# Turning retention's, attention's and the mixed result's blocks by transposing DMAs, with the mixing's first two column blocks summed pair by pair and fewer accumulating transfers

## The chip, the cores and the metric

One core of a Trainium2 chip runs the whole layer as one program. The metric is the device time of that program in microseconds (us). The profile comes from one execution of it.

## The reference, cut to what matters

The layer works on 256 tokens of 2048 features in float32: a half feed-forward (SwiGLU, 5632 wide), two token mixers side by side, a projection of their gated sum, a second half feed-forward, and a gated embedding. Only the parts that the change touches are quoted:

```python
def reference(...):
    h = layer_norm(alpha * h + 0.5 * swiglu(h, w_ffn1_gu, w_ffn1_down), ...)
    rq, rk, rv, rg, aq, ak, av, gate_r, gate_a = split(h @ w_in)
    ...
    ro = head_group_norm(retention_chunkwise(rq, rk, rv), ret_gn_g)        # 8 heads of 256
    ret_branch = (silu(rg) * ro) @ w_ret_out
    att_branch = sliding_window_attention_sinks(aq, ak, av, sinks) @ w_att_out   # 16 heads of 64
    mixed = (sigmoid(gate_r) * ret_branch + sigmoid(gate_a) * att_branch) @ w_mix_out
    h = layer_norm(alpha * h + mixed, ...)
    h = layer_norm(alpha * h + 0.5 * swiglu(h, w_ffn2_gu, w_ffn2_down), ...)
    ...
```

`swiglu(h)` is `(silu(g) * u) @ w_down`, where g and u are the two halves of `h @ w_gu`.

## The kernel before

**Products.** Every float32 operand of a large product is held as two float32r parts, a rounded one (hi) and the rest (lo). `Sum.add` (lines 387 to 396) issues three matmuls for one product of a 128x128 by a 128x512 block: lo by hi, hi by hi, hi by lo. A weight chunk is 128 x 1024 (512 KB). `Single` loads one through SyncE's queue (line 113) and makes hi by a copy on ScalarE (line 99) and lo by a subtraction on VectorE (line 100). `Folded` makes lo without VectorE: ScalarE writes hi and then minus hi (lines 163 and 164), and an accumulating DMA that GpSimd issues adds the raw weights to that (line 165). `Seven` forms a product of two chunks with seven block products in place of eight, for which VectorE forms sums of the weights; `Prepared` is the same with sums that were formed earlier and stored away. One chunk of a plain product occupies TensorE with 12 matmuls, a `Seven` with 21.

**The order of the weights.** `plan` lists the chunks in the order of use. `fill` (line 280) runs after each chunk is used up: it has chunks made while under 45 matmuls of work stand ready, and loaded while under 90 are under way, as far as the room in SBUF goes. A stage's order is a string of letters: P is a pair of `Single` chunks, F is a `Single` and a `Folded`, S is a `Seven`, D a `Prepared`. `gu_units` (line 874) gives the order of each of the eleven groups of a feed-forward's first product. In the first feed-forward groups 1 to 10 are `FFSSFSSF`. In the second, groups 6, 8, 9 and 10 are `FFSSFSSP`, groups 4, 5 and 7 begin with `FF` and hold D, groups 1 to 3 hold no F.

**Side work.** Small jobs stand in a list, `side`. After each chunk `run_side` takes one job from it, so a job n places down the list is issued n chunks later. Engines take their own instructions in the order of issue, and SyncE's queue does the same with its loads.

**Turns.** A product needs its left operand with features on the partitions. Four stages turn a result from tokens on partitions to that form.
- A feed-forward's activations (`turned`, line 929) go by a DMA. ScalarE parts the float32 words into two planes of 16 bits (line 935), SyncE issues a transposing DMA of 16 blocks of 128x128 (line 939), and ScalarE joins the two planes to float32 again (line 948). The DMA is issued at the next chunk and the joining three chunks later.
- Retention turns each head by four TensorE transposes against an identity (line 1268, tile `rt`). ScalarE and VectorE read the result from PSUM (lines 1279 and 1280) and write the two parts `rett`. One list of side jobs for two heads has ten places.
- Attention turns the weights of two heads by six such transposes (line 1387, tile `at`) four chunks after the scores (tile `as`), and ScalarE copies them out (line 1390). `att3` multiplies them with the values (tile `ao`, lines 1403 and 1404). For the last pair of heads it comes seven chunks after the scores.
- The mixed result (`sig`) is turned by four times four transposes for each half (line 1470, tile `mxt`). Each is split into `mixt`, the left operand of the mixing's product `mo`. The first half is turned beside the second half's retention product (`mr1`). The second half is turned beside the beginning of `mo`.

**Mixing.** The product `mo` has four column blocks of 512. Each runs through all 16 blocks of features before the next begins, 8 chunks for each column block. The two accumulators of a block are read once it is done (line 1509).

Of the kernel before, what the change touches and what calls it, by code (L numbers as in the profile page):

```python
# [8 lines left out]
F32 = mybir.dt.float32  # L9
# [35 lines left out]
AHEAD_SLOTS = 32  # L45

# [10 lines left out]
def layer(ctx: ExitStack, tc: tile.TileContext, io):  # L57
# [90 lines left out]
    class Folded:  # L148
# [11 lines left out]
        def make(self):  # L160
            c = self.chunk
            c.make_hi()
            act.copy(c.hi, c.raw)
            act.mul(c.lo, c.hi.bitcast(F32), -1.0)
            pool.dma_start(c.lo, c.raw, accum_op=ALU.add)  # L165

# [752 lines left out]
    def ffn(name, i, ht, norm, keep, residual, keepers, away):  # L919
# [9 lines left out]
        def turned(j, v):  # L929


            words = slot([P, 2, 2, 512], U16, f"{name}w{j}")
            of_v = v.bitcast(U16).rearrange("p t (n h) -> p h t n", h=2)
            for h in range(2):
                act.copy(words[:, h], of_v[:, h])
            moved = slot([P, 2, 2, 4, P], U16, f"{name}m{j}")

            def turn():
                sync.dma_start_transpose(
                    moved.rearrange("p h t k n -> p (h t k) n"), words.rearrange("p h t n -> p (h t n)")  # L940
                )

            def joined():
                raw = slot([P, 4, S], F32, f"{name}a{j}")
                raws.append(raw)
                of_raw = raw.bitcast(U16).rearrange("p k (t n h) -> p h t k n", t=2, h=2)
                for h in range(2):
                    act.copy(of_raw[:, h], moved[:, h])

            later(0, turn)  # L950
            later(3, joined)
# [165 lines left out]
    gate_keys = lambda b: lambda n, p: ("w_in_f2", 29 + 4 * b + 2 * n, p)  # L1117
    ret_keys = lambda b: lambda n, p: ("w_ret2", 4 * b + 2 * n, p)

    def plan_mixers():  # L1120
        plan_tokens(("w_rv", 0), KD)
        for grp in range(8):
            plan_features([("w_in_f", grp)], KD)
        for blk in range(1, 4):
            plan_tokens(("w_rv", blk), KD)
        for grp in range(8, 16, 2):
            plan_tokens(("w_in_f2", grp), KD)
        plan_tokens(("w_av",), KD, nk=4)
# [10 lines left out]
        for blk in range(4):  # L1139
            plan_tokens(("w_mix", blk), KD)  # L1140
# [7 lines left out]
    def mixers(ht, norm, residual, keepers, away):  # L1148
# [48 lines left out]
        ret_t = [None] * HR  # L1197
        gate_v = [None] * HR
# [43 lines left out]
        def ret2b(h):  # L1242
            def f():
# [3 lines left out]
                o = half(f"ron{h}")  # L1247
# [4 lines left out]
                keep["o", h] = o  # L1252

            return f

        def ret2c(h):
            def f():
                o = keep["o", h]
                dve.tensor_tensor(o, o, gate_v[h], ALU.mult)
            return f  # L1260

        def ret3(h):
            def f():
                o = keep.pop(("o", h))
                ps = bank(f"rt{h}").rearrange("p (a b) -> p a b", a=2)
                for e in range(2):
                    for t in range(2):
                        pe.transpose(ps[:, e, t * P : (t + 1) * P], o[:, t, e * P : (e + 1) * P], ident)
                keep["r", h] = ps
            return f  # L1270

        def ret3b(h):
            def f():
                ps = keep.pop(("r", h))
                ret_t[h] = slot([P, 2, 512], F32R, f"rett{h}")
                for e in range(2):
                    gk = gn[:, 2 * h + e : 2 * h + e + 1]
                    hi, lo = ret_t[h][:, e, :S], ret_t[h][:, e, S:]
                    act.mul(hi, ps[:, e, :S], gk)
                    dve.scalar_tensor_tensor(lo, ps[:, e, :S], gk, hi, ALU.mult, ALU.subtract)  # L1280
            return f
# [11 lines left out]
        for h in range(0, HR, 2):  # L1293
# [6 lines left out]
            for e in range(2):  # L1300
                gate_v[h + e] = g[:, :, e * DV : (e + 1) * DV]
# [79 lines left out]
        def att2(m):  # L1381
            def f():
                s = keep.pop(("p", m))
                ps = banks(f"at{m}")
                for e in range(2):
                    for j in range(3):
                        pe.transpose(ps[e][:, j * P : (j + 1) * P], s[:, e, j * P : (j + 1) * P], ident)
                pt = slot([P, 2, 384], F32, f"apt{m}")
                for e in range(2):
                    act.copy(pt[:, e], ps[e][:, :384])  # L1390
                keep["pt", m] = pt
            return f
# [71 lines left out]
        def turned(v, kk):  # L1464
            mt = slot([P, 2, 512], F32R, f"mixt{len(mix_t)}")
            mix_t.append(mt)
            ps = bank(f"mxt{len(mix_t)}").rearrange("p (a b) -> p a b", a=2)
            for j in range(2):
                for t in range(2):
                    pe.transpose(ps[:, j, t * P : (t + 1) * P], v[:, t, (kk + j) * P : (kk + j + 1) * P], ident)  # L1470
            split(mt[:, :, :S], mt[:, :, S:], ps)
# [11 lines left out]
        for b in range(2):  # L1483
# [7 lines left out]
            side.append(idle)  # L1491
            side.extend(lambda v=v, kk=kk: turned(v, kk) for v in sig[2 * b : 2 * b + 2] for kk in (0, 2))
# [9 lines left out]
        for blk in range(3):  # L1502
            if blk == 2:
                load_for_norm(1)
            ps = banks(f"mo{blk}")
            y[blk] = load_columns(residual, blk, "mixy")
            tokens_out(("w_mix", blk), KD, lhs, ps)
            for t in range(2):
                dve.scalar_tensor_tensor(y[blk][:, t], y[blk][:, t], ALPHA, ps[t], ALU.mult, ALU.add)
            block_stats(stats, y, blk)  # L1510
        y[3] = load_columns(residual, 3, "mixy")
# [318 lines left out]
```

## Time and profile before

| | us |
|---|---|
| median of 3 runs | 2260.68 (2256.12 to 2261.04) |
| the profiled execution | 2257.79 |
| its span, first to last instruction | 2255.8 |
| ScalarE busy in the span | 1366.8 (61%) |
| VectorE busy in the span | 1960.8 (87%) |

A row of a group gives the line, the engine, the operation, the tile written and those read, shapes and count, then the busy time in us and the mean time of one in ns, then the idle time of the engine before these instructions and what ended it. A row of the timeline gives the start, the duration, and in brackets an idle time before it with what ended that. A row of a stretch gives for each engine the busy time and the number of instructions, then the granted TensorE clock, the share of the 16 DMA engines in use, and GB/s. TensorE's matmuls overlap, so the cost of one is read from the distance between starts and not from its duration.

### The profile page before, as it was taken

The page shows a single profiled execution, that of the slowest core. Times are in us where ns is not written, and L with a number is a line of the kernel's source. Part 1 is how long each engine was busy: PE and PEld are TensorE (multiplying, and loading weights), DVE is VectorE, ACT ScalarE, POOL GpSimd, SP SyncE. Part 2 cuts the span into 40 slices and gives each one's busy share as a digit, 9 for nine tenths or more (in the row PEclk, how much of TensorE's full clock was granted, in tenths as well). Part 3 has the DMA queues.
Part 4 walks back from the last instruction along what each step waited for, and adds up shares of the span by engine and source line. Part 5 has one row for each costly group of instructions (what it writes and reads, how often), then busy time and mean ns, then how long its engine had stood idle before and what let it go on. Part 6 is the DMA issues. An engine that isn't in the chain of part 4 may idle for free.

```text
span 2255.8 us, 29093 instructions
## 1 busy us (share of the span) xinstructions
PE 2241.5 (99%) x10303; PEld 1857.3 (82%) x10303; DVE 1960.8 (87%) x2564; ACT 1366.8 (61%) x1607; POOL 52.6 (2%) x67
## 2 busy tenths in 40 slices
PE   9999999999999999999999999999999999999998
PEld 8888888788888888888778888888887788888887
DVE  6999989999988887888789788689998899889887
ACT  6787877766554453535556454455777677655533
POOL 0010010000000000000000000000000000000000
PEclk9999999999999999999999999999999999999999
DMA  9999999965677878775456568787999998555772
GB/s 319 257 288 250 280 274 247 276 218 181 225 284 273 282 289 287 252 240 175 139 157 229 182 214 291 274 295 260 306 292 300 299 249 265 195 210 208 290 264 74
DMA packets 265241, 557.66 MB, mean 247 GB/s; under 512 B 63100, under 2 KB 67580, under 8 KB 265096
## 3 DMA queue, kind: packets, MB, share of 16 engines
q1 hardware_dynamic: 254760, 522.82, 68.7%
q0 software_dynamic: 8352, 30.41, 7.0%
q10 hardware_dynamic: 1984, 2.58, 0.4%
q8 instruction: 81, 1.33, 0.2%
q14 instruction: 64, 0.52, 0.1%
HBM read 484.43 MB, written 29.36 MB: 228 GB/s over the span
## 4 chain that ended last, share of the span: by engine, by line
PE 90%; DMA 5%; issue 2%; DVE 2%; ACT 1%; ACTq 0%; POOLq 0%; SPq 0%; DVEq 0%
DMA lf_gu<-rf_gu 3%; PE rqk L345 3%; PE f1g L394 2%; PE f1g L396 2%; PE f1g L395 2%; PE f1u L396 2%; PE f1u L395 2%; PE f1u L394 2%; PE f2g L396 2%; PE f2g L395 2%; PE f2g L394 2%; DMA rf_gu<-in_f_gu 2%; PE f2u L396 2%; PE f2u L395 2%; PE f2u L394 2%
## 5 line engine op out<-in xcount | busy, mean ns | idle before, releaser
L100 DVE TENSOR_TENSOR lf_gu<-rf_gu,hf_gu 128x1024 fp32r<-128x1024 f32 (+1 forms) x210 | 250.2, 1208 | 15.5 <-ACT hf_gu L99 14.7
L99 ACT CAST hf_gu<-rf_gu 128x1024 fp32r<-128x1024 f32 (+1 forms) x210 | 214.4, 1038 | 33.6 <-DMA rf_gu<-in_f_gu 32.2
L100 DVE TENSOR_TENSOR lf_down<-rf_down,hf_down 128x1024 fp32r<-128x1024 f32 x150 | 178.8, 1219 | 18.4 <-ACT hf_down L99 17.2
L100 DVE TENSOR_TENSOR lw_in_f<-rw_in_f,hw_in_f 128x1024 fp32r<-128x1024 f32 x140 | 167.4, 1218 | 25.0 <-ACT hw_in_f L99 24.7
L99 ACT CAST hf_down<-rf_down 128x1024 fp32r<-128x1024 f32 x150 | 151.9, 1050 | 51.9 <-DMA rf_down<-in_f_down 22.3
L99 ACT CAST hw_in_f<-rw_in_f 128x1024 fp32r<-128x1024 f32 x140 | 140.2, 1051 | 2.9 <-PE rv L395 1.4
L99 ACT CAST huf_gu<-uf_gu 128x1024 fp32r<-128x1024 f32 x76 | 80.1, 1054 | 95.8 <-DVE uf_gu L191 94.1
L99 ACT CAST hvf_gu<-vf_gu 128x1024 fp32r<-128x1024 f32 x76 | 80.1, 1054 | 32.5 <-DVE vf_gu L193 31.5
L165 POOL DMA_DIRECT2D lf_gu<-rf_gu x58 | 50.2, 866 | 1845.9 <-DMA rf_gu<-in_f_gu 1253.0
L100 DVE TENSOR_TENSOR luf_gu<-uf_gu,huf_gu 128x1024 fp32r<-128x1024 f32 x76 | 92.5, 1217 | 0.0
L100 DVE TENSOR_TENSOR lvf_gu<-vf_gu,hvf_gu 128x1024 fp32r<-128x1024 f32 x76 | 92.5, 1217 | 0.0
L394 PE MATMUL f1g<-hf_gu,xt 128*128 128x512 f32 x232 | 90.5, 390 | 0.2 <-ACT hf_gu L99 0.2
L396 PE MATMUL f1g<-lf_gu,xt 128*128 128x512 f32 x232 | 90.5, 390 | 0.0
L395 PE MATMUL f1g<-hf_gu,xt 128*128 128x512 f32 x232 | 90.3, 389 | 0.0
L394 PE MATMUL f2g<-hf_gu,ht 128*128 128x512 f32 x214 | 83.4, 390 | 0.0
L396 PE MATMUL f2g<-lf_gu,ht 128*128 128x512 f32 x214 | 83.3, 389 | 0.0
L395 PE MATMUL f2g<-hf_gu,ht 128*128 128x512 f32 x214 | 83.3, 389 | 0.0
L396 PE MATMUL f1u<-lf_gu,xt 128*128 128x512 f32 x192 | 75.3, 392 | 2.4 <-DMA lf_gu<-rf_gu 2.4
L394 PE MATMUL f1u<-hf_gu,xt 128*128 128x512 f32 x192 | 74.7, 389 | 0.0
L395 PE MATMUL f1u<-hf_gu,xt 128*128 128x512 f32 x192 | 74.7, 389 | 0.0
L396 PE MATMUL f2u<-lf_gu,ht 128*128 128x512 f32 x168 | 66.0, 393 | 4.5 <-DMA lf_gu<-rf_gu 4.5
L394 PE MATMUL f2u<-hf_gu,ht 128*128 128x512 f32 x168 | 65.8, 391 | 0.0
(1464 smaller groups left out, 6796.5 us busy)
## 6 DMA issues: line engine op xcount, KB each, us to landing
rf_gu<-in_f_gu SPq DMA_DIRECT2D x360, 512.0 KB
rf_down<-in_f_down SPq DMA_DIRECT2D x176, 512.0 KB
rw_in_f<-in_w_in_f SPq DMA_DIRECT2D x148, 512.0 KB
lf_gu<-rf_gu POOLq DMA_DIRECT2D x58, 512.0 KB, 7.8
rw_rv<-in_w_rv SPq DMA_DIRECT2D x32, 512.0 KB
rw_ret<-in_w_ret SPq DMA_DIRECT2D x32, 512.0 KB
rw_mix<-in_w_mix SPq DMA_DIRECT2D x32, 512.0 KB
rw_pg<-in_w_pg SPq DMA_DIRECT2D x32, 512.0 KB
```

The costliest lines, as they stand in the source:

```text
L99: act.copy(dst_hi, src)
L100: (lo_engine or dve).tensor_tensor(dst_lo, src, dst_hi, ALU.subtract)
L165: pool.dma_start(c.lo, c.raw, accum_op=ALU.add)
L345: pe.matmul(ps[f], hi[:, kk, f * P : (f + 1) * P], rhs(k), start=k == 0, stop=k == n_k - 1,)
L394: pe.matmul(o, al, bh, start=first, stop=False)
L395: pe.matmul(o, ah, bh, start=False, stop=False)
L396: pe.matmul(o, ah, bl, start=False, stop=self.left == 0)
```

## The change

The DMA turn becomes a class, `Turn`, with `part` (two ScalarE copies), `move` (the transposing DMA on SyncE's queue) and `join` or `join_rows` (two ScalarE copies). Retention, attention and the mixed result use it in place of TensorE's transposes: one turn for two heads of retention (4 in all, 16 blocks each), one for two heads of attention (8, 12 blocks each), one for 512 columns of the mixed result (4, 16 blocks each). The 112 TensorE transposes of these stages are gone. In retention and the mixed result ScalarE and VectorE then read the joined tile in SBUF where they read PSUM.

In retention, `move` is issued two chunks before `join`, in attention too, and in the mixed result as well. In the feed-forwards `move` is issued one chunk later than before (`DELAY`), and the joining one chunk later too.

The mixing's first two column blocks are summed together: each pair of features is multiplied with both blocks' chunks before the next pair, with four accumulators held. Their readings come after the sixteenth chunk.

Of the `Folded` chunks 15 of 58 become `Single`. These are the last F of each of groups 1 to 10 in the first feed-forward (now `FFSSFSSP`), and in the second the first F of groups 4, 5 and 7 and of groups 6 and 8 (now `PFSSFSSP`).

```diff
+DELAY = 1
+    class Turn:
+        def __init__(self, src, name):
+            self.a, self.b = src.shape[1], src.shape[2] // P
+            self.src, self.name = src, name
+        def part(self):
+            of_src = self.src.bitcast(U16).rearrange("p a (n h) -> p h a n", h=2)
+            self.words = slot([P, 2, self.a, self.b * P], U16, "w" + self.name)
+            for h in range(2):
+                act.copy(self.words[:, h], of_src[:, h])
+        def move(self):
+            self.moved = slot([P, 2, self.a, self.b, P], U16, "m" + self.name)
+            sync.dma_start_transpose(
+                self.moved.rearrange("p h a b n -> p (h a b) n"), self.words.rearrange("p h a n -> p (h a n)")
+            )
+        def join(self, dst):
+            of_dst = dst.bitcast(U16).rearrange("p b (a n h) -> p h a b n", a=self.a, h=2)
+            for h in range(2):
+                act.copy(of_dst[:, h], self.moved[:, h])
...
-            return units_of(*((f"{plain * 2}SDSDSP", SEVEN[:3]) if j % 2 else (f"{plain * 2}SSDSSP", SEVEN)), AHEAD[j])
-        order = "FFSSFSSP" if name == "f2" else "FFSSFSSF"
+            return units_of(*((f"P{plain}SDSDSP", SEVEN[:3]) if j % 2 else (f"P{plain}SSDSSP", SEVEN)), AHEAD[j])
+        order = "FFSSFSSP" if name == "f1" or j > 8 else "PFSSFSSP"
...
-            later(0, turn)
-            later(3, joined)
+            later(DELAY, turn.move)
+            later(DELAY + 3, joined)
...
+    MIX_UNITS = [("P", p) for p in range(KD // 2)]
+    mix_keys = lambda n, p: ("w_mix", n, p)
...
-            side.append(ret2c(h))
-            side.append(ret2c(h + 1))
-            side.append(ret3(h))
-            side.append(both(ret3b(h), ret3(h + 1)))
-            side.append(ret3b(h + 1))
+            c = h // 2
+            side.extend((ret2c(c), ret3(c), ret3a(c), idle, ret3b(c)))
...
-            for j, part in ((0, att1), (1, att1b), (2, att1c), (4, att2)):
+            for j, part in ((0, att1), (1, att1b), (2, att1c), (3, att2), (4, att2a), (6, att2b)):
...
-            side.append(idle)
-            side.extend(lambda v=v, kk=kk: turned(v, kk) for v in sig[2 * b : 2 * b + 2] for kk in (0, 2))
+            t0, t1 = (Turn(v, f"mx{2 * b + n}") for n, v in enumerate(sig[2 * b : 2 * b + 2]))
+            side.extend((
+                t0.part, lambda t0=t0, t1=t1: (t0.move(), t1.part()), t1.move,
+                lambda t0=t0: split_turned(t0), lambda t1=t1: split_turned(t1),
+            ))
...
+        pm = [banks(f"mo{blk}") for blk in range(2)]
+        block("mo0", MIX_UNITS, mix_keys, lhs, None, [[Sum(pm[n][t], KD) for n in range(2)] for t in range(2)], None, before_mix)
+        for blk in range(2):
+            residual_added(blk, pm[blk])
```

`ret3`, `ret3a` and `ret3b` call `part`, `move` and `join`, `att2`, `att2a` and `att2b` do the same with `join_rows`. `split_turned` joins and then splits into two tiles of `mixt`.

More of the change, by code (lines that the diff above doesn't have):

```diff
@@ L165, in make, with join_rows @@
             pool.dma_start(c.lo, c.raw, accum_op=ALU.add)
+    class Turn:
[16 more added lines that the diff above has]
+                act.copy(of_dst[:, h], self.moved[:, h])
+        def join_rows(self, dst):
+            of_dst = dst.bitcast(U16).rearrange("p a (n h) -> p h a n", h=2)
+            for h in range(2):
+                act.copy(of_dst[:, h], self.moved[:, h].rearrange("p a b n -> p a (b n)"))
     class Seven:
@@ L929, in turned @@
         def turned(j, v):
[L932 to L941, printed above, removed]
-            def joined():
[L944 to L948, printed above, removed]
-            later(0, turn)
-            later(3, joined)
+            turn = Turn(v, f"{name}{j}")
+            turn.part()
+            def joined():
+                raws.append(slot([P, 4, S], F32, f"{name}a{j}"))
+                turn.join(raws[-1])
+            later(DELAY, turn.move)
+            later(DELAY + 3, joined)
         acts = {}
@@ L1138, in plan_mixers @@
             block_units(RET_UNITS, ret_keys(b))
-        for blk in range(4):
+        block_units(MIX_UNITS, mix_keys)
+        for blk in range(2, 4):
             plan_tokens(("w_mix", blk), KD)
@@ L1195, in mixers @@
             values(blk, ps)
[L1197 to L1198 removed]
+        ret_t, gate_v = [], []
         keep = {}
@@ L1382, in f, with att2a, att2b @@
             def f():
[L1383 to L1391, printed above, removed]
+                keep["t", m] = Turn(keep.pop(("p", m)), f"at{m}")
+                keep["t", m].part()
+            return f
+        def att2a(m):
+            return lambda: keep["t", m].move()
+        def att2b(m):
+            def f():
+                keep["pt", m] = slot([P, 2, 384], F32, f"apt{m}")
+                keep.pop(("t", m)).join_rows(keep["pt", m])
             return f
@@ L1462, in of_pairs, with split_turned @@
             return a[:, :S], a[:, S:]
[L1464 to L1471, printed above, removed]
+        def split_turned(turn):
+            raw = slot([P, 4, S], F32, f"mixr{len(mix_t)}")
+            turn.join(raw)
+            for j in (0, 2):
+                mt = slot([P, 2, 512], F32R, f"mixt{len(mix_t)}")
+                mix_t.append(mt)
+                split(mt[:, :, :S], mt[:, :, S:], raw[:, j : j + 2])
         slots_for_weights(20)
@@ L1501, in mixers, with residual_added @@
         lazy.append(sums_ahead(ahead[8:], 3, 2))
[L1502 to L1507, printed above, removed]
+        def residual_added(blk, ps):
             for t in range(2):
```

54 lines of the change are left out of this document (30 added, 24 removed).

## The prediction

> **What bounds the kernel now.** I read the page's first part, then the slices, then who waited for whom on TensorE, then the groups of the transposes on TensorE.
>
> ```profile
> span 2255.8 us, 29093 instructions
> ## 1 busy us (share of the span) xinstructions
> PE 2241.5 (99%) x10303; PEld 1857.3 (82%) x10303; DVE 1960.8 (87%) x2564; ACT 1366.8 (61%) x1607; POOL 52.6 (2%) x67
> ## 2 busy tenths in 40 slices
> PE   9999999999999999999999999999999999999998
> ```
> ```profile
> PE f2u L396 <- DMA lf_gu<-rf_gu: 4.5, 5, 1.7
> PE f1u L396 <- DMA lf_gu<-rf_gu: 2.4, 4, 1.1
> ```
>
> TensorE (PE) is busy in 2241.5 of 2255.8 us and in every slice. So the time can only come from work taken off TensorE and from its few stops. Nearly all stops inside the span are of one kind: a matmul waits for the lo part of a `Folded` chunk, which an accumulating DMA writes, nine times for 6.9 us in all. VectorE is at 87% and must stay behind TensorE. ScalarE, at 61%, has room.
>
> **The transposes on TensorE.** These are the groups that go, and four rows of the timeline round one set of four:
>
> ```profile
> L1387 PE MATMUL at<-ident,asc 128*128 128x128 f32 x48 | 6.8, 277 | 0.0
> L1268 PE MATMUL rt<-ident,ron 128*128 128x128 f32 x32 | 4.8, 272 | 0.0
> L1470 PE MATMUL mxt<-ident,sig 128*128 128x128 f32 x32 | 4.8, 272 | 0.0
> ```
> ```profile
> 1375.48 0.39 PE L396 MATMUL mo<-lw_mix,mixt 128*128 128x512 f32 x1
> 1375.71 0.60 PE L1470 MATMUL mxt<-ident,sig 128*128 128x128 f32 x4
> 1376.06 0.47 PE L394 MATMUL mo<-hw_mix,mixt 128*128 128x512 f32 x1
> 1376.38 0.39 PE L395 MATMUL mo<-hw_mix,mixt 128*128 128x512 f32 x1
> ```
>
> A row's duration overlaps the next, so I count starts. From 1375.48 to 1376.38 lie 0.90 us, in which two matmuls also begin. A matmul takes 0.23 from start to start (1375.48 to 1375.71), so two take 0.46 and four transposes 0.44 us, 0.11 each. The bare distance, 0.35 for four, gives 0.09. At 0.11 the 32 + 32 of retention and the mixed result give 7.0 us, the 48 of attention 5.3, **12.3 us** together (10.1 at 0.09). The groups' own busy times, 6.8 + 4.8 + 4.8 = 16.4, overlap their neighbours and are the upper bound. TensorE has no gap in these stages (the stretches below), so what it no longer issues comes off the end, if nothing else becomes late.
>
> **What takes their place.** ScalarE, SyncE's queue and the DMAs. The feed-forwards' turns show the prices:
>
> ```profile
> L948 ACT COPY f1a<-f1m x22: 1347/1355/1366, 70.1 to 480.9; 128x1024 uint16<-128x1024 uint16 x22
> L939 SPq DMA_TRANSPOSE f1m<-f1w x11: 1322/1874/3547, 57.5 to 468.0; - x11
> ...
> L935 ACT COPY f1w<-evw x20: 1036/1041/1044, 96.7 to 467.0; 128x1024 uint16<-128x1024 uint16 x20
> ```
> ```profile
> 905.00:1018.00 113.00, 113.00 (x621) 98.12 (x621) 95.67 (x196) 51.20 (x70) 0.00 (x0) 1.00 0.75 251
> 1030.00:1160.00 130.00, 130.00 (x684) 103.59 (x683) 98.43 (x189) 73.30 (x157) 0.00 (x0) 1.00 0.48 150
> 1325.00:1400.00 75.00, 75.00 (x347) 62.05 (x347) 67.52 (x75) 37.00 (x43) 0.00 (x0) 1.00 0.71 240
> 86.00:127.00 41.00, 41.00 (x182) 33.83 (x181) 37.40 (x46) 31.84 (x35) 3.46 (x4) 1.00 0.92 262
> 1712.00:1753.00 41.00, 39.30 (x172) 31.92 (x171) 40.11 (x49) 31.85 (x34) 3.47 (x4) 1.00 0.94 269
> 1835.00:1876.00 41.00, 41.00 (x182) 33.97 (x181) 38.59 (x47) 30.89 (x33) 2.40 (x4) 1.00 0.90 255
> ```
>
> The columns are TensorE, weight loads, VectorE, ScalarE, GpSimd, clock, DMA share and GB/s; the first three rows are retention's, attention's and the mixed result's turns. A turn of 16 blocks costs ScalarE 2 x 1.04 to part and 2 x 1.355 to join, 4.8 us; one of attention's 12 blocks three quarters, 3.6. Retention's four add 19 us, attention's eight 29, the mixed result's four 19. ScalarE is idle for 62, 57 and 38 us of these stretches, and attention's old copies out of PSUM go as well. VectorE gets no new instruction here. SyncE's queue is held 1.3 to 3.5 us by each of 16 issues (30 us at the median of 1.87), and its loads are issued up to 90 matmuls, some 20 us, ahead. So none of it fills an engine; what counts is when a turn arrives.
>
> The trace shows no row for the landing of a transposing DMA. From below it is the issue, 1.9 us. From above, the first joining started at 70.1 after the issue at 57.5 and waited for nothing, so 12.6. Of the same 512 KB, SBUF to SBUF, is the accumulating transfer, and I take its landing:
>
> ```profile
> lf_gu<-rf_gu POOLq DMA_DIRECT2D x58, 512.0 KB, 7.8
> ```
>
> The joining is issued two chunks after the DMA, 2 x 12 x 0.227 = 5.4 us. At 7.8 ScalarE then waits some 2.4 us, with the next chunks' copies queued behind it, and VectorE's subtractions after those. Chunks are made up to 45 matmuls ahead, 10.2 us. 2.4 of waiting and 2.7 of joining stay below that, so I cost it at nothing, with this cover named.
>
> Two places have a deadline of their own.
>
> ```profile
> 1372.33 1.23 DVE L1490 TENSOR_TENSOR sig<-sig,eve 128x1024 f32<-128x1024 f32 x1
> ...
> L394 PE MATMUL mo<-hw_mix,mixt x128: 389/389/481, 1370.3 to 1458.5; 128*128 128x512 f32 x128
> ...
> L99 ACT CAST mixt<-mxt x8: 578/587/595, 1332.3 to 1385.9; 128x512 fp32r<-128x512 f32 x8
> L100 DVE TENSOR_TENSOR mixt<-mxt,mixt x8: 680/686/693, 1334.0 to 1386.6; 128x512 fp32r<-128x512 f32 x8
> ...
> L1377 DVE TENSOR_SCALAR asc<-asc,asm x32: 279/318/350, 1039.9 to 1147.8; 128x128 f32<-128x128 f32 x16, 128x256 f32<-128x256 f32 x16
> L1403 PE MATMUL ao<-apt,akv x32: 379/404/431, 1061.9 to 1158.2; 128*64 128x256 f32 x32
> ```
>
> *The mixed result.* The first tile of the second half is ready at 1373.6. Parting 2.1, landing 7.8, joining 2.7, the split 0.6 + 0.7: 1387.5. The mixing begins at 1370.3 and uses it from its ninth chunk on, now at 1370.3 + 8 x 2.72 = 1392.1. That leaves 4.6 us to spare. In the old order of column blocks it would be the fifth chunk, at 1381.2, and TensorE would stand 6.3 us. So the pair order pays for the turn and brings nothing by itself; its later readings of the accumulators fall to VectorE, which in that stretch has 7.5 us free of 75.
>
> *Attention's last pair of heads.* The last normalising ends at 1148.1. Parting three quarters of 2.1 gives 1.6, landing 7.8, joining 2.0: 1159.5. TensorE's last products with the values begin at 1158.2 less what is saved. A stop of about 1.3 us; none at a landing of 1.9, 6.1 at 12.6. I take **1.3**, and nothing for the other pairs, which have at least one chunk more.
>
> **The stops.** Three of the five in the second feed-forward are at the first F of a group:
>
> ```profile
> 1676.41 0.50 PE L396 MATMUL f2u<-lf_gu,ht 128*128 128x512 f32 x1 [0.39 <-DMA lf_gu<-rf_gu]
> ...
> 1718.15 0.50 PE L396 MATMUL f2u<-lf_gu,ht 128*128 128x512 f32 x1 [1.25 <-DMA lf_gu<-rf_gu]
> ...
> 1799.90 0.39 PE L395 MATMUL f2u<-hf_gu,ht 128*128 128x512 f32 x1
> 1801.98 0.50 PE L396 MATMUL f2u<-lf_gu,ht 128*128 128x512 f32 x1 [1.69 <-DMA lf_gu<-rf_gu]
> 1802.32 0.39 PE L394 MATMUL f2u<-hf_gu,ht 128*128 128x512 f32 x1
> ```
>
> Counting 24 matmuls for P or F and 21 for S or D, these are the first units of groups 5, 6 and 8, where F becomes P. A stop costs more than its idle: 1799.90 to 1802.32 is 2.42, less two steps of 0.23 is 1.96, 0.27 over the 1.69. So 0.39 + 1.25 + 1.69 + 3 x 0.27 = **4.1 us** go. The other six (2.4 in the first feed-forward, 1.2 in the second, and 6 x 0.27, 5.2 together) are at the F between the S pairs, which stays. But there each group issues a transfer less into DMAs that are 0.92 in use. I take a third of them, **1.7**, with bounds of 0 and 5.2.
>
> What is late next is VectorE: each of the 15 chunks gives it one subtraction more, 1.2 us by the 128x1024 rows of the page:
>
> ```profile
> L100 DVE TENSOR_TENSOR lf_gu<-rf_gu,hf_gu 128x1024 fp32r<-128x1024 f32 (+1 forms) x210 | 250.2, 1208 | 15.5 <-ACT hf_gu L99 14.7
> ```
>
> A group of the first feed-forward goes from 37.4 to 38.6 of 41 us. The stretch at 1835 has that very order, `FFSSFSSP`, and 38.59, with no stop of TensorE. In the stretch at 1712, group 6, VectorE is at 40.11 of 41 already; with 1.2 more it is full. But the next groups hold D, whose sums are ready-made, and the S parts only lose lead. I cost this at 0.3, from 0 to 2 x 1.2. The one-chunk delay of the feed-forwards' DMA moves a wait off SyncE's queue and nothing onto TensorE: its results are used groups later.
>
> **The sum.** 12.3 + 4.1 + 1.7 - 1.3 - 0.3 = 16.5 us. The profiled execution took 2257.8 (span and 2.0 around it), which gives 2241.3. It lies 2.9 below the median of the three runs, 2260.7, which gives 2244.2. The runs fall on both sides of the profiled one, so I take the middle, **2243**.
>
> **The rivals.**
> - *The stops come back elsewhere.* VectorE, 1.2 us later at up to 15 places, or the F between the S pairs, keeps TensorE waiting where the first F did, and the landing at attention's end is late. For it: VectorE at 40.11 of 41. Against: its surplus comes back one group later. Then only the transposes count, less 6 us in all: 12.3 - 6 = 6.3, some 2254; without the 6 it is 2248. Chance 0.22.
> - *Slower: the joining starves the weights.* ScalarE waits in its queue for each landing, and the hi copies wait behind. TensorE stops when the wait and a joining of 2.7 and one copy of 1.0 pass the 10.2 us of work made ahead, that is at a wait over 6.5 us, a landing over 11.9 after the issue. The trace only bounds it by 12.6 (above), taken beside weight loads at 0.9 of the DMAs. At 14 us each of 16 turns would stop TensorE for 2.1, 34 us: 2260.7 - 18.1 + 34 = 2277. Against it: the twin transfer lands in 7.8, and these stretches use 0.5 to 0.75 of the DMAs. Chance 0.08. [...]
> - *It is hidden.* Less than 4.5 us (0.2%, about what a measurement of this kernel can tell from no change) comes off, since new short stops at the turns eat the 12 us. That needs 0.7 us at each of 16 turns. Chance 0.06.
>
> The forecast has the other 0.64. Faster by over 0.2%: 0.64 and the 0.22 together, 0.86; within 0.2%: 0.06; slower: 0.08. The range ends below where all stops go and nothing new comes: 2257.8 - 12.3 - 4.1 - 5.2 = 2236. Above it ends at the first rival's 2254, and what lies past that holds less than 2 in 10.
>
> **What would show it.** TensorE with 10303 - 112 = 10191 instructions and about 2228 us busy; no `rt`, `at`, `mxt`; three fewer of the five waits of `f2u` for `lf_gu`; no wait of `mo` for `mixt`; at most a short one of `ao` for `apt`; ScalarE's waits for the new transposing DMAs near 2 us. Wrong it would be if TensorE waited for hi or lo parts of `w_in_f`, `w_ret` or `w_mix`, or for VectorE's `lvf_gu` in groups 6 and 8.

## The result, and the profile after

The changed kernel takes 2252.48 us (median of 9 runs, 2251.64 to 2256.44) against 2258.99 for the kernel before on the same chip (9 runs, 2256.12 to 2261.04). The ratio is 0.9976, interval 0.9966 to 0.9986. It is 6.5 us faster, where 16.5 were forecast: the direction was right, and 2252 lies inside the range, but the size was far off. The profiled execution took 2251.64.

The page of the changed kernel begins so:

```profile
span 2249.9 us, 28922 instructions
## 1 busy us (share of the span) xinstructions
PE 2230.0 (99%) x10191; PEld 1845.7 (82%) x10191; DVE 1976.5 (88%) x2575; ACT 1406.5 (63%) x1640; POOL 39.7 (2%) x52
```

TensorE has its 112 instructions less and is busy 11.5 us less, close to the 2228 forecast. The span is only 5.9 shorter, so some 5.6 us of new standing time have appeared. Who waited for whom on TensorE, in the kernel after (total us, times, longest):

```profile
PE f1u L428 <- DMA lf_gu<-rf_gu: 4.1, 6, 1.8
PE ao L1423 <- ACT apt L197: 3.2, 2, 2.5
PE f2u L428 <- DMA lf_gu<-rf_gu: 2.5, 3, 1.8
...
PE f27s L428 <- DVE luf_gu L102: 0.8, 1, 0.8
PE ro L1253 <- DVE rsp L102: 0.5, 1, 0.5
PE mr1s L428 <- DVE luw_ret L102: 0.4, 1, 0.4
PE pln L1635 <- DVE plnst L1633: 0.2, 1, 0.2
PE f27s L428 <- DVE lvf_gu L102: 0.2, 1, 0.2
PE mr1s L428 <- DVE lvw_ret L102: 0.2, 1, 0.2
```

Before, `f1u` waited 2.4 and `f2u` 4.5 us. Now it is 4.1 and 2.5: the stops on accumulating transfers have moved from one feed-forward to the other. The waits of `ao` (attention's weights by the values), `ro` (retention's output), and `mr1s` and `f27s` (sums of `Seven` chunks, in the second half's retention product and in group 7 of the second feed-forward) are new.

Taken from the first TensorE instruction of each stage to that of the next, the stages changed as follows (us, less before; the forecast's 1.7 is shared out by the stops it stood for, and the last three columns are experiments below). Each column is one execution, and that of the orders alone, 2262.15 us, lies 3.3 above the median of its runs: a difference of a microsecond or two in one row is within what executions differ by.

| stage | forecast | after | orders alone | turns alone | best version |
|---|---|---|---|---|---|
| first feed-forward's product (`f1g`, `f1u`) | -1.1 | +2.1 | +2.8 | +0.8 | -3.2 |
| retention, attention, mixed result | -11.0 | -8.4 | +0.1 | -8.2 | -6.9 |
| second feed-forward's product (`f2g`, `f2u`) | -4.4 | -0.1 | +1.3 | +5.6 | -2.9 |
| the rest | 0 | +0.4 | -0.1 | 0 | +0.3 |

### The profile page after: what moved, and what is told of

The parts are those of the page before. It is cut to its first block, busy times and chain, and to the rows that moved or that the text cites. A ratio compares the mean times of both kernels' runs of the same rounds, so it can differ in the third digit from the quotient of the medians.

```text
span 2249.9 us, 28922 instructions
## 1 busy us (share of the span) xinstructions
PE 2230.0 (99%) x10191; PEld 1845.7 (82%) x10191; DVE 1976.5 (88%) x2575; ACT 1406.5 (63%) x1640; POOL 39.7 (2%) x52
## 4 chain that ended last, share of the span: by engine, by line
PE 75%; DVE 10%; DMA 6%; ACT 4%; issue 4%; SPq 0%; ACTq 0%; DVEq 0%; POOLq 0%
DMA lf_gu<-rf_gu 3%; PE rqk L377 3%; PE f1g L428 2%; PE f1g L427 2%; PE f1g L426 2%; PE f2g L427 2%; PE f2g L426 2%; PE f2g L428 2%; PE f1u L428 2%; PE f1u L427 2%; PE f2u L428 2%; PE f1u L426 2%; DVE lw_in_f L102 2%; PE f2u L427 2%; PE f2u L426 2%
## 5 line engine op out<-in xcount | busy, mean ns | idle before, releaser
L102 DVE TENSOR_TENSOR lf_gu<-rf_gu,hf_gu 128x1024 fp32r<-128x1024 f32 (+1 forms) x225 | 267.7, 1210 | 20.5 <-ACT hf_gu L101 19.7
L101 ACT CAST hf_gu<-rf_gu 128x1024 fp32r<-128x1024 f32 (+1 forms) x225 | 228.5, 1039 | 33.3 <-DMA rf_gu<-in_f_gu 32.9
L167 POOL DMA_DIRECT2D lf_gu<-rf_gu x43 | 37.3, 868 | 1852.8 <-DMA rf_gu<-in_f_gu 1240.9
```

Of the source, the lines that this page charges most:

```text
L101: act.copy(dst_hi, src)
L102: (lo_engine or dve).tensor_tensor(dst_lo, src, dst_hi, ALU.subtract)
```

## The experiments

**Which part brought what.** Four kernels take the change apart. *Turns only*: the changed kernel with the old unit orders and the feed-forward's turn undelayed.

```diff
-DELAY = 1
+DELAY = 0
-        order = "FFSSFSSP" if name == "f1" or j > 8 else "PFSSFSSP"
+        order = "FFSSFSSP" if name == "f2" else "FFSSFSSF"
...
```

> The kernel before with the three turns by DMA and the pair order of the mixing alone: old orders, DELAY 0. By the prediction's sum 11.0 us off: 2248. By the trace of the changed kernel the transposes give 13.4 and new stops in retention, attention and the retention product take 5.1: 2250 to 2252, all of the measured gain. Theory C would have this one faster than the kernel with old orders and the delay by 2 us or more.

Measured: 2253.76, ratio 0.9978 (0.9968 to 0.9987). *Orders only*: the kernel before with the new unit orders.

```diff
-        order = "FFSSFSSP" if name == "f2" else "FFSSFSSF"
+        order = "FFSSFSSP" if name == "f1" or j > 8 else "PFSSFSSP"
...
```

> The kernel before with the new orders alone (43 Folded), TensorE's transposes and the block order of the mixing kept. By the prediction's sum the stops give 5.5 us: 2253. Theory A: 4 go at the first F and as much comes back at the F between the S pairs and at the S parts of group 7: 2257 to 2260. Theory B: 2260 or more.

Measured: 2258.84, ratio 0.9998 (0.9990 to 1.0007). So the turns alone bring 5 us, nearly all there is, and 15 accumulating transfers fewer bring nothing. *Old orders*: the changed kernel with the old orders, still delayed.

```diff
-        order = "FFSSFSSP" if name == "f1" or j > 8 else "PFSSFSSP"
+        order = "FFSSFSSP" if name == "f2" else "FFSSFSSF"
...
```

> The changed kernel with the 15 chunks made Folded again (58 in all). Theory A, the stops of the F between the S pairs come from a lead of some 7.5 us that VectorE's work on the S parts fixes, whatever the other chunks do: the stops at the first F of the second feed-forward's groups come back (3 to 4 us), the others stay within 2 us; 2254 to 2257. Theory B, VectorE pays for the 15 chunks and makes things late: this kernel is faster than the changed one, 2247 to 2250.

Measured: 2266.39, ratio 1.0027 (1.0016 to 1.0037), slower than before and outside both forecasts. *No delay*: the changed kernel with the turn undelayed, and nothing else.

```diff
-DELAY = 1
+DELAY = 0
```

> The changed kernel with the feed-forwards' transposing DMA issued at the next chunk again (DELAY 0). Theory C, the delayed DMA falls in with the accumulating transfer of the F between the S pairs and makes it land late: the first feed-forward's stops fall from 4.7 us to 3 or less and the second's at that F from 3.9 to 2, 2248 to 2250. Theory A: no change beyond 1 us, 2251 to 2253.

Measured: 2252.15, ratio 0.9964 (0.9952 to 0.9977), the same as with the delay. The delay costs 12.6 us with the old orders and nothing with the new ones. In the waits of the run with old orders the reason can be read:

```profile
PE f1u L428 <- DMA lf_gu<-rf_gu: 10.2, 10, 2.4
PE f2u L428 <- DMA lf_gu<-rf_gu: 5.2, 6, 1.9
```
```profile
118.09 2.57 ACT L192 COPY f1a<-mf 128x1024 uint16<-128x1024 uint16 x2
...
122.56 1.06 ACT L166 ACTIVATE lf_gu<-hf_gu 128x1024 fp32r<-128x1024 f32 x1
...
123.98 0.88 POOL L167 DMA_DIRECT2D lf_gu<-rf_gu  x1 [16.04 <-ACT lf_gu L166]
...
132.15 0.50 PE L428 MATMUL f1u<-lf_gu,xt 128*128 128x512 f32 x1 [2.36 <-DMA lf_gu<-rf_gu]
```

Delayed by a chunk, the joining (two copies, 2.7 us of ScalarE) stands in ScalarE's queue ahead of the copies that the last F of the next group needs before its transfer can be issued. That F's transfer then starts 6.2 us ahead of its use in the mean, in place of 8.4 in the run of the turns only. Its stops in the first feed-forward are 6.7 of the 10.2 us above, and cost TensorE 11.9 us with what it loses after each. With the new order the last unit is a P, so nothing stands there. What the new orders pay for is the delay; neither brings anything without the turns.

**Where the stops come from.** In the changed kernel six of the nine transfers that are waited for in the first list of waits are at the F between the S pairs of the first feed-forward, and the other three at the same place of the second. One transfer less in each group was to make them land sooner. It did not; of the DMA issues between 53 and 465 us, the median landing is the last column, first of the kernel before, then of the kernel after:

```profile
lf_gu<-rf_gu POOLq DMA_DIRECT2D x38, 512.0 KB, 7.4
```
```profile
lf_gu<-rf_gu POOLq DMA_DIRECT2D x28, 512.0 KB, 7.7
```

The two medians are not of the same places, since the last F of each group, which landed soonest (6.6 us in the mean), is gone. At the F between the S pairs alone the mean landing is 7.4 us before and after.

Two of these transfers in the kernel after, both issued 7.6 to 7.8 us ahead of their first use, show what makes the difference. The first is issued at 188.97. Its first packet (q0) begins at 190.40; the weight loads (q1) that were under way are nearly over. The DMA queues up to then, and from then on:

```profile
q1 hardware_dynamic: 121, 0.22, 40.5%
lf_gu<-rf_gu POOLq DMA_DIRECT2D x1, 512.0 KB, 5.3
```
```profile
q0 software_dynamic: 144, 0.52, 93.1%
q1 hardware_dynamic: 52, 0.11, 11.1%
```

It lands after 5.3 us and nobody waits. The second is issued at 312.22, while SyncE's queue puts out five loads that stood behind a transposing DMA:

```profile
305.43 4.46 SPq L185 DMA_TRANSPOSE mf<-wf  x1
309.99 3.85 SPq L115 DMA_DIRECT2D rf_gu<-in_f_gu  x5
```
```profile
q1 hardware_dynamic: 1142, 1.41, 89.0%
lf_gu<-rf_gu POOLq DMA_DIRECT2D x1, 512.0 KB, 9.5
```
```profile
q0 software_dynamic: 141, 0.52, 66.9%
q1 hardware_dynamic: 287, 0.56, 39.4%
```
```profile
319.59 0.39 PE L427 MATMUL f1u<-hf_gu,xt 128*128 128x512 f32 x1
321.79 0.50 PE L428 MATMUL f1u<-lf_gu,xt 128*128 128x512 f32 x1 [1.81 <-DMA lf_gu<-rf_gu]
```

For 5.2 us the engines carry 1.41 MB of q1 (loads, and what is left of the transposing DMA) and not one packet of the transfer; then it takes its own 3.9 us. It lands 9.5 us after the issue, and TensorE stands 1.81 us. Over all 43 transfers of that trace the packets take 3.1 to 5.3 us from first to last, while the first comes 1.4 to 5.2 us after the issue. What differs between these two is where loads fall. All 19 traces together bear that out. Leave aside transfers that stand behind one of their own kind: where SyncE's queue issued a load between 1.55 us before the transfer and 0.75 after it, the first packet came after 3.7 us (median of 310), and after 1.8 us (263) where it did not; in the traces of before and after alone 3.5 us (36) and 1.5 us (27). (The two bounds were chosen on the changed kernel's trace.) Five kernels tried to give these transfers more time.

*A plain chunk in that place* (P between the S pairs, F last; undelayed):

```diff
...
+        order = "FFSSPSSF" if name == "f1" else "FFSSPSSP" if j > 8 else "PFSSPSSP"
```

> The kernel without the delay, with the F between the S pairs made plain instead: FFSSPSSF in the first feed-forward, PFSSPSSP in groups 6 and 8 and FFSSPSSP in 9 and 10 of the second (39 Folded). Theory A, that F alone has too short a lead: the first feed-forward's stops fall from 4.7 us to under 1, the second's from 5.0 to 1 or 2 (VectorE at the S parts), 2244 to 2247. Theory B, VectorE is the wall and the stops only move: S parts or last F stop TensorE for as much, 2251 to 2253.

Measured: 2254.71, ratio 0.9977 (0.9969 to 0.9986). The stops went, but for one, to the last F, whose lead is 7.0 us where it was 8.4 in the run of the turns only. VectorE's one subtraction more ahead of it is the likely reason; no run shows it alone.

*More work made ahead* (57 and 102 matmuls in place of 45 and 90, undelayed):

```diff
...
-                        slots_for_weights(24)
+                        slots_for_weights(24, 57, 102)
...
-                    slots_for_weights(AHEAD_SLOTS - j)
+                    slots_for_weights(AHEAD_SLOTS - j, 57, 102)
```

> The kernel without the delay, with chunks made up to 57 matmuls ahead in place of 45 in both feed-forwards' first products (loaded up to 102). Theory A, the lead of that F is set by VectorE's unbroken work on the S parts, behind which ScalarE's copies wait in their queue: no gain, 2251 to 2253. Theory D, the planner's 45 matmuls set it: it grows by 2.7 us and the stops at that F go, 2243 to 2246.

Measured: 2295.39, ratio 1.0158 (1.0135 to 1.0180), much slower, and outside both forecasts. Against the undelayed run the lead of the F between the S pairs of the first feed-forward rose by 0.4 us in the mean, its landing by 2.0, and VectorE's parts came late in the second feed-forward as well.

*One S ahead of the F in place of two* (undelayed):

```diff
...
-        order = "FFSSFSSP" if name == "f1" or j > 8 else "PFSSFSSP"
+        order = "FFSFSSSP" if name == "f1" or j > 8 else "PFSFSSSP"
```

> The changed kernel with the joining undelayed, and the second pair of F chunks behind one S chunk instead of two: FFSFSSSP in fused stage 1 and in the last two f2 groups, PFSFSSSP in f2 groups 6 and 8. Theory (the F that stands behind S chunks has its accumulating transfer issued a fixed time ahead of its use, because its ScalarE copies stand behind the S chunks' copies, which wait for VectorE; one S less in front gives it about 2 us more): the lead of that F rises from 7.6 to 9 us or more, its stops fall from 4.7 us to under 1 in f1 and from 3.5 to under 1 in f2, and the kernel takes 2245 to 2249 us, if the three S chunks in a row behind it do not wait for VectorE. Rival 1 (VectorE has no slack, so the stops only change place): stops of 4 to 6 us on the later S chunks, 2251 to 2255 us. Rival 2 (the landing time stretches by as much as the lead): the same sum of stops on the F chunk, 2252 us.

Measured: 2295.27, ratio 1.0164 (1.0144 to 1.0183): the theory fell. The waits and the landing of this run:

```profile
PE f1u L428 <- DMA lf_gu<-rf_gu: 23.7, 10, 3.4
PE f2u L428 <- DMA lf_gu<-rf_gu: 12.0, 4, 4.8
```
```profile
lf_gu<-rf_gu POOLq DMA_DIRECT2D x43, 512.0 KB, 9.0
```

The lead stayed at 7.7 us; so the S chunks ahead do not set it, and what does is not settled. But now every one of these 14 transfers is issued 0.2 to 0.5 us before a load's first packets, waits 4.2 to 6.0 us for its own first packet and lands after 9.0 to 11.1. Behind the issue of one of them, from 148.82 to 154.20, the engines carried 0.99 MB of q1 and not one packet of the transfer. A stop now and then has become one in each group. Where the loads come from can be read too: each of the 14 is issued 3.3 to 3.5 us after a feed-forward's transposing DMA, in the undelayed run 7.9 to 8.3, so that it meets the loads that stood behind that DMA in SyncE's queue. In the changed kernel's first feed-forward, the four transfers at this place that come less than 7 us after such a DMA (groups 7 to 10) all make TensorE stop; of the other six two do, for 0.4 and 0.5 us. It is not the whole of it: four of ten stop in the undelayed run too, at 7.9 us and more, and no run moved that DMA alone with everything else kept.

*The rest last.* This takes the transfers as they are and moves their first use. Of an F chunk's twelve matmuls the four that read the rest (lo) are issued after the other eight:

```diff
...
-                    tokens_chunk(u.chunk, 2 * p, lhs, [sums[t][n] for t in range(2)], (0, 1))
+                    if kind == "F" and n == 1:
+                        for part in (Sum.add_high, Sum.add_low):
+                            for kk in range(2):
+                                for t in range(2):
+                                    part(sums[t][1], half_of(lhs(2 * p + kk), t), u.chunk.columns(kk))
+                    else:
+                        tokens_chunk(u.chunk, 2 * p, lhs, [sums[t][n] for t in range(2)], (0, 1))
```

> The changed kernel, with the matmuls of each F chunk in another order: the 8 that need only the rounded part (made by ScalarE) first, the 4 that need the rest (finished by the accumulating transfer) last; nothing else is moved. The first use of the rest falls 6 matmuls of 0.2268 us later, 1.36 us. Theory (a stop is the time by which a transfer, held up behind a weight load in the DMA engines, lands after its first use): every stop on an F chunk gets shorter by 1.36 us or goes; the 6 of fused stage 1 (5.86 us) leave 0.8, the 6 of fused stage 2 (4.2 us) leave 0.8, and the kernel takes 2243 to 2246 us. Rival (VectorE has no slack: what TensorE doesn't wait for at an F chunk it waits for at an S chunk): stops of luf and lvf take their place, 2249 to 2253 us.

Measured: 2247.76, ratio 0.9949 (0.9937 to 0.9962), 4.7 us under the changed kernel and between the two forecasts. Its waits:

```profile
PE ao L1444 <- ACT apt L197: 3.2, 2, 2.5
...
PE f27s L443 <- DVE lf_gu L102: 1.3, 1, 1.3
PE f2u L431 <- DMA lf_gu<-rf_gu: 1.3, 2, 1.0
PE f27s L443 <- DVE luf_gu L102: 0.8, 1, 0.8
PE f1u L431 <- DMA lf_gu<-rf_gu: 0.7, 2, 0.5
```

`f1u` falls from 4.1 to 0.7, and its stage is 4.65 us shorter, as the theory said. In the second feed-forward `f2u` falls too, but `f27s` waits for VectorE instead: there the rival was right, and of the 3.4 us that the theory promised only 1.0 came off. The same edit on the kernel before:

> The kernel before with that order of the F chunks' matmuls alone. Theory (stops are late landings, whatever the number of the transfers): of the 11 stops that the trace of before shows, 9.8 us in all, the F chunks' fall by 1.36 us each and leave 1.0; the kernel takes 2249 to 2252 us, as much off as the whole change brought. Rival (VectorE has no slack): 2256 to 2259 us.

Measured: 2254.10, ratio 0.9977 (0.9967 to 0.9986), between the two forecasts again. This edit of the matmuls' order, with no instruction more or fewer, is worth as much to the kernel before as the whole change. In its trace the second feed-forward's product is 4.7 us shorter; the first is 0.8 longer, with one transfer late by 2.3 us.

**Attention's late pair.** The last two heads' output (`ao`) waits 2.52 us for the joined weights (`apt`). Some rows of VectorE, ScalarE, SyncE's queue and TensorE in the timeline of the changed kernel:

```profile
1130.59 0.50 PE L1354 MATMUL as<-akv,aq 64*128 64x128 f32 x4
1131.75 1.22 DVE L511 TENSOR_TENSOR gaf1w<-ht 128x1024 f32<-128x1024 f32 x1
1135.68 1.22 DVE L102 TENSOR_TENSOR gaf1l<-sums,gaf1h 128x1024 fp32r<-128x1024 f32 x1 [1.12 <-ACT gaf1h L101]
1138.86 1.02 DVE L1359 SCALAR_TENSOR_TENSOR asc<-as,mask 128x384 f32<-128x384 f32 x2
1141.43 0.21 ACT L1376 ACTIVATE aes<-aes 128x4 f32<-128x4 f32 x1 [3.10 <-DVE aes L1369]
1147.03 1.56 ACT L181 COPY wat<-asc 128x768 uint16<-128x768 uint16 x2
1148.62 1.46 SPq L185 DMA_TRANSPOSE mat<-wat  x1
1152.52 1.95 ACT L197 COPY apt<-mat 128x768 uint16<-128x768 uint16 x2 [0.29 <-DMA mat<-wat]
1154.52 0.66 PE L1423 MATMUL ao<-apt,akv 128*64 128x256 f32 x4 [2.52 <-ACT apt L197]
```

The transposing DMA is issued at 1148.62, and ScalarE's joining, which waited for it, begins at 1152.52: a landing of 3.9 us, half of the 7.8 taken. What is late lies before it. VectorE begins with the scores 8.3 us after TensorE has begun them, for the most part behind the gate's forms (`gaf1`). Four kernels tried to bring it forward, by these lines:

```diff
-        begin = [0, 5, 10, 15, 20, 24, 28, 32, 38, 39]
+        begin = [0, 4, 8, 12, 17, 21, 25, 29, 36, 39]
...
-            for j, part in ((0, att1), (1, att1b), (2, att1c), (3, att2), (4, att2a), (6, att2b)):
+            for j, part in ((0, att1), (1, att1b), (2, att1c), (3, att2), (4, att2a), (5, att2b)):
...
-                if c == 0 and j >= 2:
+                if c == 1 and j >= 2:
```

| edit | us | ratio and interval | what came |
|---|---|---|---|
| late pairs four chunks apart, begun up to 3 chunks sooner (`begin = [0, 4, 8, 12, 17, 21, 25, 29, 36, 39]`) | 2259.61 | 1.0003 (0.9995 to 1.0012) | three stops of `ao`, 6.7 us |
| from the fifth pair on one chunk sooner, ahead of the forms (`begin = [0, 5, 10, 15, 19, 23, 27, 31, 38, 39]`), joined one chunk sooner (`(5, att2b)`), undelayed | 2257.29 | 0.9996 (0.9987 to 1.0004) | `ao` 1.7, but the gate's product waits 4.4 us for a weight's copy |
| the forms two chunks later (`c == 1` for `c == 0`) | 2254.79 | 0.9983 (0.9974 to 0.9992) | `ao` still 3.7 |
| the best version below, forms two chunks later, last pair one chunk sooner (31 for 32) | 2245.39 | 0.9938 (0.9926 to 0.9951) | `ao` still 4.0, none of it at the last pair, 2.8 at the sixth |

> The changed kernel with attention's pairs of heads begun earlier, four or five chunks apart (at 0, 4, 8, 12, 17, 21, 25, 29, the values of the last two at 36 and 39), so that no pair's scores fall in with the forms of the gate on VectorE and the last joining has four chunks. If that is what made the last pair late, both stops of TensorE before the values go, 3.5 us: 2248 to 2250. If the landing or the two copies themselves are too long, the stops stay and it is 2252.

> The changed kernel with attention's pairs begun at chunks 0, 5, 10, 15, 19, 23, 27, 31 (from the fifth on one chunk earlier, so that the scores of the sixth and the eighth stand ahead of the gate's split forms in VectorE's queue), and each joining one chunk sooner (ahead of the next pair's exponentials in ScalarE's queue). Theory (attention's 3.5 us of stops come from the forms and the exponentials that stand in the queues, not from the transfer): the stops of ao fall from 3.2 to under 0.5 us, and the kernel takes 2249 to 2250 us. Rival (the transfer's 3.9 us and its two rearrangements make the chain too long for pairs 4 chunks apart, as in the run with pairs begun earlier): stops of ao of 3 to 7 us remain, 2252 to 2259 us.

> The changed kernel, with the gate's two sets of split forms issued two chunks later, behind the scores of attention's sixth and eighth pair on VectorE's queue. Theory (the last pair is late since its scores stand behind the forms): the scores start about 3 us sooner, the last pair's stop of 2.7 us falls under 0.5, the other of 0.8 stays, and the kernel takes 2249 to 2250 us. Rival (the forms' copies on ScalarE then wait for VectorE in front of the weights' copies, as in the run with the pairs begun ahead of the forms): TensorE waits 2 us or more for a weight's rounded part in the gate stage, 2252 to 2256 us.

> The kernel with joining undelayed, the rest last and the forms two chunks later, and attention's last pair begun one chunk sooner (31 in place of 32). Theory (the last pair is late since its chain of about 24 us, from scores to output, begins too late, wherever the forms stand): its stop of 2.6 us goes, the other of 1.2 stays, and the kernel takes 2243.5 to 2245 us. Rival (VectorE's and ScalarE's queues are full there, as with all pairs one chunk sooner): the gate stage gets a wait for a weight's rounded part instead, 2246 to 2252 us.

None of them helped. Where the forms stand behind the scores, their copies on ScalarE wait for VectorE (5.5 us for each of the two sets in the second of these kernels, 1.5 and 1.2 in the changed one), and the weights' copies stand behind them. Each place that was tried shifted the wait, to another pair or another product, and took little off it. So it is not the forms' place alone. The DMA's landing is a part of the late chain, 3.9 us of it. That ScalarE's and VectorE's queues are full of mutual waits there fits all four, but no run took work out of them, so this stays argued; nor did one take out the DMA.

**Both together.** Two kernels joined failed edits: the plain chunk with the earlier pairs, and one S ahead with the pairs ahead of the forms.

> The plain F between the S pairs, no delay, and attention's pairs begun earlier, together. By theory A and the earlier pairs the two gains add: 2241 to 2244. By theory B only the second remains: 2248 to 2250.

> Both edits of the two runs beside it. Theory: their gains add, as they lie in different stages (fused stages 1 and 2 against the attention's): 2243 to 2247 us. Rival (VectorE has no slack, or the transfer is too slow): 2251 to 2262 us.

Measured: 2260.89 (1.0012, 1.0003 to 1.0020) and 2304.92 (1.0205, 1.0191 to 1.0219). Two joined the one that held: the rest last, undelayed and with the forms later, and the same with the forms where the change has them.

> The changed kernel with the joining undelayed, the F chunks' matmuls in the order of the run with the rest last, and the gate's forms two chunks later. Theory: the F chunks' stops go (f1 4.7 us, f2 3.5 us) and the last pair's, 2241 to 2244 us. Rivals as in the two runs beside it: 2249 to 2256 us.

> The changed kernel with the joining undelayed and the F chunks' matmuls in the order with the rest last; the gate's forms stay where the change has them. Theory (the undelayed joining leaves VectorE's queue ahead in fused stage 2, and the forms' place brings nothing): 2245.5 to 2247 us, no more than the run with the forms later. Rival (the forms' later place was worth something there): 2248 us or more.

Measured: 2246.72 (0.9945, 0.9932 to 0.9959) and **2245.30** (0.9938, 0.9924 to 0.9951), the best of all: the changed kernel with the rest last and the turn undelayed. Its waits:

```profile
PE ao L1444 <- ACT apt L197: 3.2, 2, 2.6
...
PE f27s L443 <- DVE luf_gu L102: 0.8, 1, 0.8
PE f1u L431 <- DMA lf_gu<-rf_gu: 0.5, 1, 0.5
...
PE f2u L431 <- DMA lf_gu<-rf_gu: 0.5, 1, 0.5
```

With the stops on accumulating transfers down to 1.0 us the kernel stands 14.1 us under the kernel before, near the 2243 of the forecast. The forecast's sum thus needed an edit that the change doesn't make.

## Why the prediction was right or wrong

- **The transposes: right.** Retention, attention and the mixed result are 8.4 us shorter. In them stand the new waits of `ao`, `ro` and `mr1s`, 4.3 us idle by the rows above and 5.1 with what each costs in restarting. So 13.5 us came off for 112 transposes, 0.12 each; 12.3 at 0.11 was forecast. The turns alone measured -5.1 us net.
- **The stops: wrong, the step that failed.** 4.1 and 1.7 us were to go, and VectorE to give back 0.3. The two products together became 2.0 us longer: 7.6 us of the 10.3 by which the profiled execution's 2251.64 misses its forecast of 2241.3. The three stops at the first F of groups 5, 6 and 8 did go. But the F between the S pairs of that feed-forward rose from 1.8 to 3.8 us and an S chunk of group 7 from 0.2 to 1.9, and the first feed-forward's F from 3.7 to 5.9 (each with what restarting costs). The reason given, that fewer transfers land sooner in DMAs that are 0.92 in use, was not so: the median went from 7.4 to 7.7 us, and at that F the mean stayed at 7.4. A transfer's landing goes with the loads issued close to it (the first packet after 3.7 us in the median with one, after 1.8 without), and the edits shift those. That the orders bring nothing is shown by the run of the orders alone, at 0.9998. The 0.3 for VectorE also left out that a lead can shrink. In groups 6 and 8, which now begin with a P and so have one subtraction more in front, the transfer of the F between the S pairs starts 5.9 and 6.0 us ahead of its use, before 7.5 and 7.7 (5.75 with the orders alone, where its two stops made 1.5 us). That they made only 0.5 us in the changed kernel is luck: the two landed in 6.3 and 6.0 us.
- **Attention's last pair: right place, wrong size.** 1.3 was forecast, 2.5 measured, and 0.7 at another pair. The landing was half of what was taken. But "1158.2 less what is saved" was then used as 1158.2. After the change TensorE arrives at 1152.0, 6.2 us sooner (5.9 sooner than the 1157.9 at which the last pair's first product began; 1158.2 is a later one), while the parting of the normalised weights begins at 1147.0, 1.1 sooner than the 1148.1 taken for it: the chain runs on VectorE and ScalarE, which the change did not make faster. Two errors partly cancelled, which is luck.
- **Retention and `mr1s`: costed at nothing, 1.1 us of idle time.** VectorE is late there by a few tenths, as it was not before.
- **The mixed result: right.** No wait of `mo` for `mixt`.
- **The delay: right with these orders alone.** It was put at nothing, and 2252.15 without it against 2252.48 with it is nothing.
- **The rivals.** "The stops come back elsewhere" is what happened, by the F between the S pairs, by attention's end (though not by a late landing there) and by VectorE a little. Its 2248 to 2254 holds the result. The chance of 0.22 was too small, since the trace of before showed landings but not what made them differ. "The joining starves the weights" did not come: in attention ScalarE waited 0.8 us in all for the landing of these DMAs. But its mechanism, a joining ahead of copies that TensorE needs soon, cost 12.6 us where the old orders were left with the delay.

## What to carry to other kernels

A stop on a transfer is a race between its landing and its first use. Before costing the stop away by having fewer transfers, look in the trace at what its packets wait for; if that is other traffic, put the use later, which costs no instruction (here six matmuls, 1.36 us, worth 5 to 7). When the busiest engine gets faster, take its saving off the deadline of every chain that runs on other engines, and keep that number through the sum.

## What was not expected of the hardware

- **An accumulating transfer's first packet came up to 5.2 us after its issue.** In the changed kernel it came 1.4 us after the issue at the earliest, with no load issued in the 1.5 us before, and 5.2 us after it where loads were issued close by and q1 moved 1.41 MB meanwhile (6.0 in the run with one S ahead); once begun, both queues shared the engines (66.9% and 39.4% above). Why they did not share them before the first packet is not settled.
- **TensorE's granted clock fell to 0.56 after a stop of 2.64 us.** In the best version the last `ao` stops for that long, up to 1149.29. A stretch before it and two behind it read (TensorE, its loads, VectorE, ScalarE, GpSimd, granted clock, DMA share, GB/s):

```profile
1141.00:1146.00 5.00, 5.00 (x27) 3.66 (x26) 3.57 (x6) 5.00 (x6) 0.00 (x0) 1.00 0.33 64
1150.60:1153.00 2.40, 2.40 (x10) 1.81 (x7) 2.32 (x5) 2.09 (x5) 0.00 (x0) 0.56 0.73 253
1153.00:1156.00 3.00, 3.00 (x15) 2.44 (x14) 2.93 (x5) 2.98 (x4) 0.00 (x0) 1.00 0.10 38
```

  At a clock of 0.56 a step takes 0.43 us (1151.79 to 1152.22) in place of 0.23, and the stop costs an estimated 1.7 us more: with the clock at 0.60 in the 1.5 us from 1149.00, 0.4 x 1.5 + 0.44 x 2.4. Behind the changed kernel's stop of 2.52 us the clock stayed at 1.00:

```profile
1154.50:1156.00 1.50, 1.48 (x11) 1.09 (x12) 0.59 (x1) 1.43 (x3) 0.00 (x0) 1.00 1.06 352
```

  In the run with the rest last, whose longest stop of `ao` is 2.5 us by its waits above, the clock was 0.64 in 1149.80:1151.00, 0.50 in 1151.00:1153.30 and 0.99 in 1153.50:1156.00. So the length of the stop does not seem to separate them; what does is not shown.
- **A transposing DMA of 12 blocks lands in 3.9 us**, but its issue holds SyncE's queue 1.5 us there and 4.5 us for 16 blocks in the first feed-forward (1148.62 and 305.43 above), and the loads behind it then go out in a burst (five in 3.85 us from 309.99).
